# Layer-norm and RMS-norm sums with 128 columns of ones, and the gate products' copies ahead of layer norm, in a two-layer decoder trunk

## The chip, the cores and the metric

The kernel runs on one core of a Trainium2 chip. Its engines are TensorE (PE in the profile; PEld is its weight load), VectorE (DVE), ScalarE (ACT), GpSimd (POOL) and SyncE (SP), which here only starts transfers. The metric is the device time of one execution in microseconds. The time before is 1310.84 us, the median of three runs (1309.58 to 1313.38).

## The reference, cut to what matters

Two layers over 512 tokens of width 1024, all in float32. Layer 0 mixes with a causal Conformer convolution, layer 1 with differential attention; after each mixer come a SwiGLU feed-forward part and a gated embedding.

```python
u = rms_norm(h, conv_norm_g)
a = u @ w_pw1 + b_pw1                              # 1024 -> 2048
u = a[..., :D] * sigmoid(a[..., D:])
u = depthwise_causal_conv(u, dw_w, width=31) + dw_b
u = silu(layer_norm(u, ln_g, ln_b))                # mean and variance over 1024 channels
h = h + (u @ w_pw2 + b_pw2)
h = h + swiglu(rms_norm(h, ffn_norm_g), w_gate, w_up, w_down)
gate = sigmoid(rms_norm(h, ple_norm_g) @ w_ple_gate)
h = h + gate * (p[i] @ w_ple_proj)                 # "gate products" below are p[i] @ w_ple_proj
```

`rms_norm` needs the mean square over the 1024 channels of a token, `layer_norm` the mean as well.

## The kernel before, in words

Activations lie transposed: eight chunks (c = 0 to 7) of 128 channels by 512 tokens. A float32 product is made of three products in a reduced format: every operand is split into a high part (a cast on ScalarE) and a low part (a subtraction on VectorE), and `mm3` (L153 to L157) adds low weight times high data, high weight times low data, and high times high. A weight tile of 128 x 1024 comes from memory into `wraw`, and `weight` (L137) splits it into `whi` (L148) and `wlo` (L150). `ones` is a 128 x 128 tile of ones in full float32; a product in full float32 is two matmul records in the trace.

A sum over the channels of one token runs across partitions, so TensorE does it, with ones as one of its operands. There are two ways in this kernel. In the first, 128 tokens of the data are the weights and **one** column of ones is the data: the result is a column, one sum for each token (L202 and L212 for RMS norm, L441 for layer norm). In the second, ones are the weights and 512 tokens are the data: the result is a row of sums, repeated over all partitions (L442).

The convolution part goes through the chunks in one loop (L444): two products of 24 matmuls each (`half`), the gate on ScalarE and VectorE, and then the 31 taps. Chunks 1, 3, 5, 6 go through memory into an order of four phases, and TensorE does their taps with 128-column products (L357); the result goes out through memory again (`phased_out`: copy L365, a transfer on ScalarE's queue L367, four on SyncE's L370, VectorE L375). Chunk 7 shares its taps: 8 on TensorE (L313), 8 on ScalarE and GpSimd (L393, L394), 15 on VectorE (L406), joined in L407 and L409.

Layer norm follows. `moments(c)` (L420) squares a chunk on ScalarE (L429) and adds it to a running sum of squares (L433) and a running sum (L435, called `macc`), on GpSimd for all but the last. `add_moments` (L437) then makes TensorE's sums: eight one-column products and one row product for chunk 7 and the same for the running sums. From them come 1/sigma (L523 to L525, L229, L231, L529), spread over all partitions by one product with ones (`lrow`, L532), and the mean is taken off (L537, L540, L542). Per chunk follow L549 (times 1/sigma), L550 (SiLU), L552 (high part) and L554 (low part), and `linear` multiplies by `w_pw2`, its first three output chunks side by side.

The gate products of layer 0 (`factor`, L500, and `project`, L274) depend on none of this. Eight of them, 6 matmuls each, are put around layer norm to give TensorE work: four after the last tap, two after the sums, two after `lrow`. Each takes one of the four `mm` buffers of PSUM until ScalarE has copied it out (L280).

The order of instructions on each engine is set by a scheduler that plays the program through with its own costs when the kernel is built; `issue_after` ties an instruction behind another of the same engine, and `manual_schedule` (L546) keeps the written order for a block. So a change in one place can move instructions everywhere behind it.

## Time and profile before

| | |
|---|---|
| median of the runs | 1310.84 us (1309.58 to 1313.38) |
| profiled execution | 1306.01 us |
| its span, from the first instruction to the last | 1304.2 us |
| TensorE busy | 1279.5 us (98%) |
| mean granted TensorE clock | 0.988 |
| VectorE, ScalarE, GpSimd busy | 56%, 40%, 18% |
| memory traffic over the span | 100 GB/s |

How to read it: a group or timeline row gives start, busy time, engine, line, operation and `out<-in`, then the count. In brackets stands how long the engine was idle before and what released it. Where rows of one kind follow each other, the distance of their starts is the price of one; a busy time is longer than that, since matmuls overlap. "PEclk" is the share of the full clock that TensorE was granted, so a busy TensorE at 0.50 does half the work.

### The profile page before, as it was taken

How to read it: one execution, taken by the hardware profiler on the slowest of the kernel's cores; microseconds unless marked ns; L12 is line 12 of the kernel's file. 1: busy time of each engine (PE TensorE's matmuls, PEld its weight loads, DVE VectorE, ACT ScalarE, POOL GpSimd, SP SyncE). 2: the span in 40 equal slices, each digit the busy share in tenths (PEclk: the TensorE clock that was granted, in tenths of full speed). 3: DMA queues.
4: the chain of work that ended last, by engine and by line, in shares of the span. 5: the costliest groups of instructions: out<-in, count | busy, mean ns of one | idle time of the engine just before them, and what ended most of it. 6: DMA issues, size and time to landing. Idle time of an engine off the chain costs nothing. (4 is left out here: it accounts for less than half of the span.)

```text
span 1304.2 us, 15514 instructions
## 1 busy us (share of the span) xinstructions
PE 1279.5 (98%) x5960; PEld 1061.5 (81%) x5960; DVE 733.6 (56%) x1142; ACT 523.5 (40%) x827; POOL 237.9 (18%) x200
## 2 busy tenths in 40 slices
PE   9999999999999999999999998999999999999998
PEld 8888778888888888888888886778888888888887
DVE  4997566544344434356687888846543344334445
ACT  5752354332232223254566776734322233222332
POOL 1754323000000000042435635122000000000030
PEclk8999899999999999999999998999999999999999
DMA  7555214232332233233222222213332333222231
GB/s 268 189 169 181 73 34 129 97 97 97 97 97 97 97 98 97 73 124 97 84 88 92 73 65 66 72 52 109 97 98 97 97 97 97 97 97 89 85 118 65
DMA packets 46839, 131.98 MB, mean 101 GB/s; under 512 B 5379, under 2 KB 9987, under 8 KB 46764
## 3 DMA queue, kind: packets, MB, share of 16 engines
q1 hardware_dynamic: 44640, 127.55, 30.2%
q10 hardware_dynamic: 2124, 3.43, 0.9%
q8 instruction: 47, 0.77, 0.2%
q14 instruction: 28, 0.23, 0.1%
HBM read 126.75 MB, written 4.21 MB: 100 GB/s over the span
## 5 line engine op out<-in xcount | busy, mean ns | idle before, releaser
L148 ACT CAST whi<-wraw 128x1024 fp32r<-128x1024 f32 (+2 forms) x214 | 218.7, 1027 | 564.8 <-PE mm L157 384.9
L156 PE MATMUL mm<-A,whi 128*128 128x512 f32 (+1 forms) x1096 | 426.8, 391 | 1.2 <-DVE A L554 1.2
L155 PE MATMUL mm<-A,wlo 128*128 128x512 f32 (+1 forms) x1096 | 423.8, 390 | 3.4 <-DVE wlo L150 1.9
L157 PE MATMUL mm<-A,whi 128*128 128x512 f32 (+1 forms) x1096 | 424.9, 388 | 0.0
L150 DVE TENSOR_TENSOR wlo<-wraw,whi 128x1024 fp32r<-128x1024 f32 (+2 forms) x210 | 260.1, 1242 | 76.1 <-ACT whi L148 76.0
L155 PEld LDWEIGHTS mm<-A,wlo 128*128 128x128 f32 x1096 | 206.1, 188 | 47.7 <-DVE wlo L150 2.8
L156 PEld LDWEIGHTS mm<-A,whi 128*128 128x128 f32 x1096 | 206.3, 188 | 44.5 <-DVE A L554 1.5
L157 PEld LDWEIGHTS mm<-A,whi 128*128 128x128 f32 x1096 | 206.2, 188 | 42.8 <-issue 1.0
L193 POOL TENSOR_TENSOR acc<-acc,wk 128x512 f32<-128x512 f32 x35 | 56.5, 1615 | 778.1 <-issue 660.2
L156 PE MATMUL mm<-B,whi 128*128 128x512 f32 x352 | 137.5, 390 | 0.0
L157 PE MATMUL mm<-B,whi 128*128 128x512 f32 x352 | 137.4, 390 | 0.0
L155 PE MATMUL mm<-B,wlo 128*128 128x512 f32 x352 | 137.1, 391 | 0.0
L610 DVE TENSOR_TENSOR h<-mm,h 128x512 f32<-128x512 f32 x48 | 33.0, 691 | 122.9 <-PE mm L157 122.8
L602 DVE TENSOR_TENSOR big<-mm,rb 128x512 f32<-128x512 f32 x44 | 30.4, 691 | 126.2 <-PE mm L157 126.2
L600 DVE TENSOR_TENSOR big<-mm,rb 128x512 f32<-128x512 f32 x44 | 30.4, 691 | 99.4 <-PE mm L157 93.0
L157 PEld LDWEIGHTS mm<-B,whi 128*128 128x128 f32 x352 | 66.1, 188 | 14.6
L155 PEld LDWEIGHTS mm<-B,wlo 128*128 128x128 f32 x352 | 66.1, 188 | 14.3
L156 PEld LDWEIGHTS mm<-B,whi 128*128 128x128 f32 x352 | 66.1, 188 | 14.2
L157 PE MATMUL mm<-whi,A 128*128 128x512 f32 x192 | 75.6, 395 | 0.0
L156 PE MATMUL mm<-wlo,A 128*128 128x512 f32 x192 | 75.0, 396 | 0.0
L155 PE MATMUL mm<-whi,A 128*128 128x512 f32 x192 | 74.8, 396 | 0.0
L231 POOL TENSOR_TENSOR r<-v,mhalf 128x8 f32<-128x8 f32 (+1 forms) x31 | 47.4, 1528 | 148.4 <-DVE v L229 126.0
(201 smaller groups left out, 1404.9 us busy)
## 6 DMA issues: line engine op xcount, KB each, us to landing
wraw<-in_wts SPq DMA_DIRECT2D x194, 512.0 KB, 3.5
wraw<-in_wts SPq DMA_DIRECT2D x16, 384.0 KB, 3.0
D<-in_diag SPq DMA_DIRECT2D x22, 256.0 KB, 4.7
C<-in_diag SPq DMA_DIRECT2D x16, 256.0 KB, 4.8
h<-in_xT SPq DMA_DIRECT2D x8, 256.0 KB, 5.3
bias<-scr ACTq DMA_DIRECT2D x8, 256.0 KB, 3.4
out_t<-h SPq DMA_DIRECT2D x7, 256.0 KB, 2.0
wraw<-in_wts SPq DMA_DIRECT2D x4, 256.0 KB, 4.6
```

The costliest lines, as they stand in the source:

```text
L148: A.copy(hi[:, cut], raw[:, cut])
L150: eng.tensor_tensor(lo[:, cut], raw[:, cut], f(hi[:, cut]), ALU.subtract)
L155: T.matmul(acc, al, bh, start=first, stop=False)
L156: T.matmul(acc, ah, bl, start=False, stop=False)
L157: return T.matmul(acc, ah, bh, start=False, stop=last)
L193: self.last = self.eng.tensor_tensor(self.acc, self.acc, sq, ALU.add)
L231: last_pow[0] = G.tensor_tensor(r[:, :n], v[:, :n], mhalf[:, :n], ALU.pow)
L600: V.tensor_tensor(tg, pg, rb, ALU.mult)
L602: V.tensor_tensor(tu, pu, rb, ALU.mult)
L610: V.tensor_tensor(h[m], acc, h[m], ALU.add)
```

## The change

Four things are changed.

- Every per-token sum now takes **128** columns of ones as data in place of one (`columns_sum`); the reader takes the first column of each block of 128 (`first_of`). This holds for the RMS norms and for layer norm.
- Around layer norm, five gate products stand ahead of the sums in place of four, two behind them, and the last behind `lrow`. Four ties are added: the squares of chunks 6 and 7 come behind the copy of the second gate product, the last running sums (now on GpSimd) behind GpSimd's last tap, the start of GpSimd's sum for chunk 7 behind the copy of chunk 6's taps, and one tap of chunk 7 on VectorE behind the result of chunk 6. The running sums are summed by TensorE before chunk 7, not after it. The sums of squares and of values lie in two PSUM tiles, one of them in the free `sc` buffer.
- `mm3` adds high times high second and high weight times low data last.
- The splits of `w_pw2`'s tiles are tied to other places, and the third tile has a home of its own (the buffers `C5`), so its load need not wait for a `wraw` buffer.

```diff
+    def columns_sum(t, src, first, last):
+        for b in range(4):
+            cut = slice(b * P, (b + 1) * P)
+            r = T.matmul(t[:, cut], src[:, cut], ones, start=first and b == 0, stop=last and b == 3)
+        return r
+    def first_of(t):
+        return t.rearrange("p (b k) -> p b k", b=4)[:, :, 0]
...
         T.matmul(acc, al, bh, start=first, stop=False)
-        T.matmul(acc, ah, bl, start=False, stop=False)
-        return T.matmul(acc, ah, bh, start=False, stop=last)
+        T.matmul(acc, ah, bh, start=False, stop=False)
+        return T.matmul(acc, ah, bl, start=False, stop=last)
...
-                for b in range(4):
-                    T.matmul(
-                        t[:, b : b + 1], sq[:, b * P : (b + 1) * P], ones[:, 0:1],
-                        start=c + b == 0, stop=c == NC - 1 and b == 3,
-                    )
-            return rsqrt_cols(t[:, 0:4], 4, 1.0 / D)
+                columns_sum(t, sq, c == 0, c == NC - 1)
+            return rsqrt_cols(first_of(t), 4, 1.0 / D)
...
             if j == a:
-                A.activation(pacc, tap(j), AF.Identity, scale=wt(c, j), bias=col("dw_b", c))
+                with tc.issue_after(last_out[0].ins) if alone else nullcontext():
+                    A.activation(pacc, tap(j), AF.Identity, scale=wt(c, j), bias=col("dw_b", c))
...
         for j in range(b + 1, KW):
-            V.scalar_tensor_tensor(sum_, tap(j), wt(c, j), sum_, ALU.mult, ALU.add)
+            with tc.issue_after(last_shift[0].ins) if alone and j == KW - 4 else nullcontext():
+                V.scalar_tensor_tensor(sum_, tap(j), wt(c, j), sum_, ALU.mult, ALU.add)
...
         sq = sums["sq"] = wk()
-        A.activation(sq, y[c], AF.Square)
+        with tc.issue_after(last_factor[0].ins) if c > NC - 3 else nullcontext():
+            A.activation(sq, y[c], AF.Square)
         if c == NC - 1:
             return
-        eng = G if c < NC - 2 else V
-        eng.tensor_tensor(sums["acc"], sums["acc"], sq, ALU.add)
-        if c > 1:
-            eng.tensor_tensor(macc, y[1] if c == 2 else macc, y[c], ALU.add)
+        with tc.issue_after(last_pool[0].ins) if c == NC - 2 else nullcontext():
+            G.tensor_tensor(sums["acc"], sums["acc"], sq, ALU.add)
+            if c > 1:
+                G.tensor_tensor(macc, y[1] if c == 2 else macc, y[c], ALU.add)
 
     def add_moments(a, b, first, last):
-        for k in range(8):
-            src = (b if k < 4 else a)[:, k % 4 * P : (k % 4 + 1) * P]
-            last_moment[0] = T.matmul(sums["cols"][:, k : k + 1], src, ones[:, 0:1], start=first and k == 0, stop=last and k == 7)
+        columns_sum(sums["mcols"], a, first, last)
         T.matmul(sums["mean"], ones, a, start=first, stop=last)
+        last_moment[0] = columns_sum(sums["cols"], b, first, last)
...
-    for _ in range(4):
+    for m in range(5):
         factor(last_tap)
+        if m == 1:
+            last_factor[0] = last_copy[0]
...
-        add_moments(y[NC - 1], sums["sq"], True, False)
-        add_moments(macc, sums["acc"], False, True)
+        add_moments(macc, sums["acc"], True, False)
+        add_moments(y[NC - 1], sums["sq"], False, True)
...
-    for _ in range(2):
-        factor(last_product)
...
+            if c == 1:
+                factor(last_product)
...
-    linear(NC, z, add_conv, 3, first=(None, last_add[0], scaled[1]))
+    linear(NC, z, add_conv, 3, split={0: (last_add[0], None), 3: third}, home=("C5", 2))
```

How the change moves instructions is shown at three places, all around layer norm. The lines of the changed kernel are some 10 to 17 higher: L156 to L158 is `mm3`, L173 the column sums, L454 the row sums.

**TensorE, layer norm's sums.** `mm_1347` and `mm_1302` are gate products (the fourth before, the fifth now; only the last matmul of it is shown), `B_241` and `B_257` are chunk 7, `acc` is the running sum `macc`, `B_94` the running sum of squares, `wk` the squares of chunk 7. Before:

```order
L157 MATMUL mm_1347<-wtl_299,whi_1306 128x512
L441 MATMUL tp_1318<-ones_70,wk_1303 128x1 x4
L441 MATMUL tp_1318<-ones_70,B_241_1276 128x1 x4
L442 MATMUL tp_1317<-B_241_1276,ones_70 128x512
L441 MATMUL tp_1318<-ones_70,B_94_404 128x1 x4
L441 MATMUL tp_1318<-ones_70,acc_153 128x1 x4
L442 MATMUL tp_1317<-acc_153,ones_70 128x512
```

Now:

```order
L158 MATMUL mm_1302<-wtl_300,whi_1247 128x512
L173 MATMUL sc_1364<-ones_70,acc_153 128x128 x4
L454 MATMUL tp_1363<-acc_153,ones_70 128x512
L173 MATMUL sc_1364<-ones_70,B_257_1333 128x128 x4
L454 MATMUL tp_1363<-B_257_1333,ones_70 128x512
L173 MATMUL tp_1362<-ones_70,B_94_404 128x128 x4
L173 MATMUL tp_1362<-ones_70,wk_1360 128x128 x4
```

The sums start with the running sum, and the squares of chunk 7 come last.

**ScalarE, from chunk 7's taps to the gate products' copies.** `wk_1253` and `wk_1310` are the sum that GpSimd builds for chunk 7, `C_240` and `C_256` its last tap, `mm_1163` are chunk 6's taps, `B_228` is chunk 6, and the copies into `D` are those of the gate products. Before:

```order
L365 COPY big_1226<-mm_1163 128x512
L393 ACTIVATE C_240_1273<-C_226_1223,C_61_275 128x512
L367 DMA po_1228<-big_1226 128x512
L429 ACTIVATE wk_1299<-B_228_1230 128x512
L280 COPY D_254_1319<-mm_1320 128x512
L429 ACTIVATE wk_1303<-B_241_1276 128x512
L280 COPY D_256_1328<-mm_1329 128x512
```

Now:

```order
L375 COPY big_1226<-mm_1163 128x512
L402 ACTIVATE wk_1310<-C_226_1223,vec_63,C_61_275 128x512
L443 ACTIVATE wk_1352<-B_211_1103 128x512
L377 DMA po_1228<-big_1226 128x512
L405 ACTIVATE C_254_1324<-C_226_1223,C_61_275 128x512
L405 ACTIVATE C_255_1327<-C_226_1223,C_61_275 128x512
L405 ACTIVATE C_256_1330<-C_226_1223,C_61_275 128x512
L286 COPY D_239_1265<-mm_1266 128x512
L286 COPY D_241_1274<-mm_1275 128x512
L443 ACTIVATE wk_1356<-B_228_1230 128x512
```

The copy and the transfer of chunk 6 stand earlier, the start `wk_1310` of GpSimd's sum stands later (before, it was the first of ScalarE's instructions for chunk 7), and the first two copies of gate products are ahead of chunk 6's square.

**GpSimd, the same stretch.** Before:

```order
L435 TENSOR_TENSOR acc_153<-acc_153,B_211_1103 128x512
L394 TENSOR_TENSOR wk_1253<-wk_1253,C_234_1255 128x512
L394 TENSOR_TENSOR wk_1253<-wk_1253,C_235_1258 128x512
L433 TENSOR_TENSOR B_94_404<-B_94_404,wk_1295 128x512
L394 TENSOR_TENSOR wk_1253<-wk_1253,C_236_1261 128x512
L394 TENSOR_TENSOR wk_1253<-wk_1253,C_237_1264 128x512
L394 TENSOR_TENSOR wk_1253<-wk_1253,C_238_1267 128x512
L394 TENSOR_TENSOR wk_1253<-wk_1253,C_239_1270 128x512
L394 TENSOR_TENSOR wk_1253<-wk_1253,C_240_1273 128x512
L231 TENSOR_TENSOR r_268_1397<-v_267_1395,mhalf_71 128x4
```

Now:

```order
L406 TENSOR_TENSOR wk_1310<-wk_1310,C_255_1327 128x512
L406 TENSOR_TENSOR wk_1310<-wk_1310,C_256_1330 128x512
L449 TENSOR_TENSOR acc_153<-acc_153,B_228_1230 128x512
L447 TENSOR_TENSOR B_94_404<-B_94_404,wk_1356 128x512
L237 TENSOR_TENSOR r_271_1407<-v_270_1405,mhalf_71 128x4
```

Chunk 6's two running sums, which VectorE made before, are now behind the seven additions of chunk 7 on GpSimd.

More of the change, by code (lines that the diff above doesn't have):

```diff
@@ L135, in trunk, with weight @@
     loaded = [None]
-    def weight(n=1024, pieces=1, between=(), eng=V, after=None):
+    def weight(n=1024, pieces=1, between=(), eng=V, after=(None, None), home=None):
         i = wnext[0]
         wnext[0] += 1
-        raw = sb([P, 1024], "wraw", 2)
+        raw = sb([P, 1024], *(home or ("wraw", 2)))
         hi = sb([P, 1024], "whi", 4, F32R)
@@ L147, in weight @@
                 between[k]()
-            A.copy(hi[:, cut], raw[:, cut])
-            with tc.issue_after(after.ins) if after else nullcontext():
+            with tc.issue_after(after[1].ins) if after[1] else nullcontext():
+                A.copy(hi[:, cut], raw[:, cut])
+            with tc.issue_after(after[0].ins) if after[0] else nullcontext():
                 eng.tensor_tensor(lo[:, cut], raw[:, cut], f(hi[:, cut]), ALU.subtract)
@@ L200, in columns_of_chunks @@
                 A.activation(sq, h[c], AF.Square)
-                for b in range(4):
-                    T.matmul(
-                        t[:, b : b + 1], sq[:, b * P : (b + 1) * P], ones[:, 0:1],
-                        start=c + b == 0, stop=c == NC - 1 and b == 3,
-                    )
-            return rsqrt_cols(t[:, 0:4], 4, 1.0 / D)
+                columns_sum(t, sq, c == 0, c == NC - 1)
+            return rsqrt_cols(first_of(t), 4, 1.0 / D)
         def columns(self):
             t = tp()
-            for b in range(4):
-                T.matmul(t[:, b : b + 1], self.acc[:, b * P : (b + 1) * P], ones[:, 0:1], start=True, stop=True)
-            return rsqrt_cols(t[:, 0:4], 4, 1.0 / D)
+            columns_sum(t, self.acc, True, True)
+            return rsqrt_cols(first_of(t), 4, 1.0 / D)
         def diagonal(self):
@@ L279, in project @@
             step()
-        A.copy(o, acc)
+        last_copy[0] = A.copy(o, acc)
         return o
+    last_copy = [None]
     y = []
@@ L287, in trunk @@
     last_tap = [None]
+    last_out = [None]
+    last_shift = [None]
+    last_pool = [None]
     rb = None
@@ L364, in phased_out @@
         o = big()
-        A.copy(o, accs[c])
+        last_out[0] = A.copy(o, accs[c])
         d = dram.tile([P, S], F32, tag=f"po{c}", name=f"po{c}")
@@ L393, in other_taps @@
                 A.activation(pr, tap(j), AF.Copy, scale=wt(c, j))
-                G.tensor_tensor(pacc, pacc, pr, ALU.add)
+                last_pool[0] = G.tensor_tensor(pacc, pacc, pr, ALU.add)
         yc = sb([P, 2, S], f"B{c}", 1)
@@ L491, in trunk @@
             moments(c - 3)
-    pe_taps(NC - 1)
-    other_taps(NC - 1)
-    for c in range(NC - 3, NC):
-        moments(c)
     pp = []
+    pw = [weight(), weight()]
     def factor(after):
@@ L510, in factor @@
             pp.append(project(ph, m, pw[m // 4], o))
-    pw = [weight(), weight()]
-    sums["mean"], sums["cols"] = tp(), tp()[:, 0:8]
-    for _ in range(4):
+    pe_taps(NC - 1)
+    for m in range(5):
         factor(last_tap)
+        if m == 1:
+            last_factor[0] = last_copy[0]
+    other_taps(NC - 1)
+    for c in range(NC - 3, NC):
+        moments(c)
+    sums["cols"], sums["mean"], sums["mcols"] = tp(), tp(), sc()
     with tc.issue_after(last_product[0].ins):
-        add_moments(y[NC - 1], sums["sq"], True, False)
-        add_moments(macc, sums["acc"], False, True)
+        add_moments(macc, sums["acc"], True, False)
+        add_moments(y[NC - 1], sums["sq"], False, True)
     for _ in range(2):
@@ L522, in trunk @@
     vs = sb([P, P // 2], "v8", 2)[:, :8]
-    V.tensor_scalar(vs, sums["cols"], 1.0 / D, None, ALU.mult)
+    V.tensor_scalar(vs[:, 4:8], first_of(sums["mcols"]), 1.0 / D, None, ALU.mult)
     V.tensor_tensor(vs[:, 4:8], vs[:, 4:8], vs[:, 4:8], ALU.mult)
-    V.tensor_tensor(vs[:, 0:4], vs[:, 0:4], vs[:, 4:8], ALU.subtract)
+    V.scalar_tensor_tensor(vs[:, 0:4], first_of(sums["cols"]), 1.0 / D, vs[:, 4:8], ALU.mult, ALU.subtract)
     r = rsqrt_cols(vs[:, 0:4], 4, 1.0)
@@ L548, in trunk, with linear @@
             if c < NC:
-                scaled.append(V.tensor_tensor(y[c], y[c], lrow, ALU.mult))
+                V.tensor_tensor(y[c], y[c], lrow, ALU.mult)
                 A.activation(y[c], y[c], AF.Silu, scale=col("ln_g", c), bias=col("ln_b", c))
                 z.append((sb([P, S], f"A{2 * c}", 1, F32R), sb([P, S], f"A{2 * c + 1}", 1, F32R)))
-                A.copy(z[c][0], y[c])
+                hi = A.copy(z[c][0], y[c])
             if c >= 2:
-                V.tensor_tensor(z[c - 2][1], y[c - 2], f(z[c - 2][0]), ALU.subtract)
-    def linear(n_in, src, consume, group0=1, before=None, after=None, first=(None,) * 3):
+                lo = V.tensor_tensor(z[c - 2][1], y[c - 2], f(z[c - 2][0]), ALU.subtract)
+            if c == 1:
+                factor(last_product)
+            if c == 3:
+                third = lo, hi
+    def linear(n_in, src, consume, group0=1, before=None, after=None, split={}, home=None):
         m = 0
@@ L561, in linear @@
             g = group0 if m == 0 else 1
-            ws = [weight(n_in * P, after=first[i] if m == 0 else None) for i in range(g)]
+            ws = [weight(n_in * P, after=split.get(m, (None, None)), home=home if m + i == 2 else None) for i in range(g)]
             accs = [mm() for _ in range(g)]
```

6 lines of the change are left out of this document (3 added, 3 removed).

## The prediction

> **What bounds the kernel now.** I read the page first, then the table by stage, then TensorE's timeline where that table shows a slow clock or idle time.
>
> ```profile
> span 1304.2 us, 15514 instructions
> PE 1279.5 (98%) x5960; PEld 1061.5 (81%) x5960; DVE 733.6 (56%) x1142; ACT 523.5 (40%) x827; POOL 237.9 (18%) x200
> PEclk8999899999999999999999998999999999999999
> ```
>
> TensorE is the bound: 1279.5 of 1304.2 us. Only three things can be gained: its 24.7 us of idle time, the slices in which its clock is below 9, and work taken off it. The table by stage (columns: length, busy time of PE, PEld, DVE, ACT, POOL, then clock and memory) says where the first two lie.
>
> ```profile
> 30.00:125.00 95.00, 95.00 (x526) 81.91 (x525) 82.62 (x100) 45.58 (x62) 54.84 (x42) 1.00 0.53 172
> 153.00:174.00 21.00, 19.32 (x66) 14.24 (x65) 8.81 (x14) 10.01 (x19) 8.28 (x6) 0.68 0.10 29
> 174.00:640.00 466.00, 465.60 (x2055) 383.39 (x2056) 228.16 (x278) 156.43 (x202) 40.13 (x28) 1.00 0.30 96
> 640.00:870.00 230.00, 216.15 (x1128) 182.43 (x1126) 177.81 (x461) 149.91 (x336) 92.81 (x89) 0.98 0.22 71
> 800.00:805.00 5.00, 1.83 (x10) 1.01 (x8) 4.91 (x12) 4.60 (x12) 1.43 (x3) 0.98 0.09 26
> 805.00:810.00 5.00, 1.92 (x7) 1.67 (x8) 4.62 (x16) 2.47 (x8) 2.63 (x2) 0.50 0.70 236
> 815.00:820.00 5.00, 2.41 (x17) 1.95 (x15) 4.37 (x9) 3.72 (x7) 1.95 (x1) 1.00 0.50 150
> ```
>
> The feed-forward stretch has nothing to give. The losses are layer norm (153 to 174: a clock of 0.68 means that 21 x 0.32 = 6.7 us were lost, 13.4 us at half speed), attention (640 to 870, 13.9 us idle, 8.8 of them in the three rows after 800), and a first one, where the norm of the input is summed:
>
> ```profile
> 19.71 3.40 PE L202 MATMUL tp<-ones,wk 128*128 128x1 f32 x30
> 22.97 0.65 PE L155 MATMUL mm<-A,wlo 128*128 128x512 f32 x1
> 23.42 3.41 PE L202 MATMUL tp<-ones,wk 128*128 128x1 f32 x16
> 26.69 0.77 PE L156 MATMUL mm<-A,whi 128*128 128x512 f32 x1
> 30.12 0.40 PE L155 MATMUL mm<-A,wlo 128*128 128x512 f32 x1
> 23.00:24.00 1.00, 1.00 (x6) 0.91 (x6) 0.00 (x0) 0.81 (x1) 0.00 (x0) 0.56 0.06 25
> ```
>
> Thirty one-column records take 22.97 - 19.71 = 3.26 us, 0.109 each. After them the clock halves although TensorE was busy all the time, and sixteen more take 23.42 to 26.69, 0.204 each. So the clock does not follow the busy time; a stretch of one-column products counts as rest.
>
> **The change part by part.**
>
> *128 columns for one.* The trace has products of 128 columns in full float32, the taps L357, and of 512 columns, L313:
>
> ```profile
> 130.29 4.18 PE L357 MATMUL mm<-C,D 128*128 128x128 f32 x36
> 134.30 1.95 PE L357 MATMUL mm<-C,C 128*128 128x128 f32 x16
> L357 PEld LDWEIGHTS mm<-C,D 128*128 128x128 f32 x40 | 4.8, 192 | 0.1
> 138.32 7.03 PE L313 MATMUL mm<-C,D 128*128 128x512 f32 x16
> 144.79 0.79 PE L155 MATMUL mm<-wth,wlo 128*128 128x512 f32 x1
> 146.57 0.39 PE L155 MATMUL mm<-wth,wlo 128*128 128x512 f32 x1
> 149.07 0.39 PE L157 MATMUL mm<-wtl,whi 128*128 128x512 f32 x1
> ```
>
> Each L357 record has a weight tile of its own, as the sums have, and 36 take 4.01 us: 0.111. So a sum with 128 columns costs what one with one column costs; 136 records (64 of the first norm, 32 of layer norm, 40 of the other norms) times 0.002 is 0.3 us. And the row of 30 to 125, in which three more such runs of taps lie (chunks 1, 3 and 5), has a clock of 1.00, so I expect 128-column sums to keep it. From 22.97 to 30.12 the first norm now takes 7.15 us for one product, sixteen sum records and eight products. A reduced product is (149.07 - 146.57)/11 = 0.227. At full clock that is 9 x 0.227 + 16 x 0.111 = 3.8 us. **Gain 3.3 us.** It arrives at layer norm only if VectorE keeps up: in 30 to 125 TensorE never waits and VectorE has 12.4 us free, so I count it whole.
>
> [...]
>
> *Layer norm.* I lay the changed order over the old times, as if the first norm had not moved.
>
> ```profile
> 151.49 0.50 PE L155 MATMUL mm<-wth,wlo 128*128 128x512 f32 x1 [2.03 <-ACT D L280]
> 154.07 1.87 PE L441 MATMUL tp<-ones,wk 128*128 128x1 f32 x8 [0.72 <-ACT wk L429]
> 174.40 0.50 PE L156 MATMUL mm<-A,whi 128*128 128x512 f32 x1 [1.19 <-DVE A L554]
> 137.93 2.55 ACT L393 ACTIVATE C<-C,C 128x512 f32<-128x512 f32 x4
> 142.12 0.57 ACT L365 COPY big<-mm 128x512 f32<-128x512 f32 x1
> 143.90 0.33 ACTq L367 DMA_DIRECT2D po<-big  x1
> 150.34 0.63 ACT L429 ACTIVATE wk<-B 128x512 f32<-128x512 f32 x1 [5.78 <-DVE B L375]
> 150.87 0.57 ACT L280 COPY D<-mm 128x512 f32<-128x512 f32 x1
> 137.94 10.26 DVE L406 SCALAR_TENSOR_TENSOR sc<-C,C,sc 128x512 f32<-128x512 f32 x13
> 149.21 1.09 DVE L375 SCALAR_TENSOR_TENSOR B<-B,vec,shrow 128x512 f32<-128x512 f32 x1 [1.01 <-DMA B<-po]
> 138.71 2.63 POOL L394 TENSOR_TENSOR wk<-wk,C 128x512 f32<-128x512 f32 x2 [2.15 <-ACT C L393]
> 142.54 6.72 POOL L394 TENSOR_TENSOR wk<-wk,C 128x512 f32<-128x512 f32 x5
> 141.30 1.28 POOL L433 TENSOR_TENSOR B<-B,wk 128x512 f32<-128x512 f32 x1
> ```
>
> The 2.03 us came from ScalarE: its copy L280 stood behind the square of chunk 6, which waited for VectorE and a transfer. Now two copies are ahead of that square. ScalarE does four taps (to 139.8), the copy of chunk 6's taps (140.4), the start of GpSimd's sum (0.7: 141.1) and a square (141.7); then the transfer goes out, 2.2 us earlier, and as it took 149.21 - 143.90 = 5.3 us, chunk 6 is there at 147.0. The first two copies are done by 148.1, before the fourth and fifth product need their buffers (149.3 on), so five products run without a wait. The first three took 144.79 to 149.07 + 0.23, two more are 12 x 0.227: 152.0.
>
> What is late next is GpSimd: its sum for chunk 7 starts at 141.1 instead of 138.7. Seven additions at 1.34 and a square's at 1.28 end at 151.8, and `macc` (1.28) is ready at 153.1, the sum of squares at 154.4. VectorE: ten taps to 145.8, chunk 6 from 147.0 to 148.1, four taps at 0.79 to 151.3, L407 after GpSimd at 151.8, L409: chunk 7 at 153.1. So TensorE waits **1.1 us** at the head of the sums, with the two gate products and all that follows queued behind. Then 0.9 for four columns of `macc`, 0.8 for its row (L313: 6.47/16 = 0.40 a record), 0.9 and 0.8 for chunk 7, 0.9 and 0.9 for the squares: 158.4. Two gate products of 6 x 0.227 end at 161.1.
>
> ```profile
> 162.81 0.17 DVE L523 TENSOR_SCALAR v<-tp 128x8 f32<-128x8 f32 x1 [8.32 <-PE tp L441]
> 164.71 1.28 ACT L529 ACTIVATE wk<-ident,r 128x128 f32<-128x128 f32 x4 [8.29 <-POOL r L231]
> 169.22 1.88 DVE L549 TENSOR_TENSOR B<-B,tp 128x512 f32<-128x512 f32 x3 [0.84 <-PE tp L532]
> 169.95 0.82 ACT L550 ACTIVATE B<-B,vec 128x512 f32<-128x512 f32 x1 [1.00 <-DVE B L549]
> ```
>
> The chain from sums to spread took 162.81 to 165.99, 3.2 us; two of its four small steps on VectorE now need only `macc` and chunk 7, done before. 158.5 + 2.9 = 161.4, and a gate product's copy holds ScalarE to 160.3 before it, so 161.6: a wait of **0.5 us**. Spread to 162.4; last gate product to 163.8. Chunk 0 needs L549 (0.73 to its SiLU, by the rows), 0.72 and 0.62 from 162.7 on: 164.8, a wait of **1.0 us**. The low part of chunk 0 is done 0.7 later, and is used after six products (1.4 us): the 1.19 us before 174.40 is gone. The three weight splits cost nothing: they now lie in the 8.32 us in which VectorE was idle (without that cover 1.2 us each).
>
> In the old order the three low-weight products of this group were done when TensorE went on at 174.40; now they are at 164.8 + 0.7 = 165.5. **Gain 8.9 us**: 6.7 of the clock, 3.9 of old waits (2.03, 0.72, 1.19) less 2.6 of new ones, and 0.9 that I take to lie in the changes between kinds of products, which are longer at half clock. Later chunks come every 1.4 us on ScalarE and are used every 2.0 us.
>
> *mm3's order and the third tile's home.* No row in 174 to 640 shows a wait for a moving low part, so 0. But the scheduler has replayed the attention part: the end of attention has the same steps, with the projection's products before or after their neighbours. There the trace can't say. A wait there is about 2.5 us (three rows with 8.8 us), and a slow stretch behind it costs 1.7 us: the clock was halved for 13.4 us in layer norm and from 23.1 to just before 30.12, about 6.8, so I estimate steps of 3.4 us. One such wait less or more makes -4.2 to +4.2 us. I take 0, as the tail begins with the same list of stages left.
>
> Sum: -3.3 - 8.9 + 0.2 = **-12.0 us** (0.1 of the 0.3 lies in the terms). The profiled execution, 1306.0 us with 1.8 around its span, becomes 1294; the runs' median lies 4.8 above that execution, and the change is carried over to it: 1310.8 - 12 = **1299 us**.
>
> **The rivals.**
>
> 1. *The clock follows idle time, not the width.* Then the waits start the slow stretches and the sums only lie in them. [...] For it: 2.03 us idle stood ahead of the fall at 152.9. Against it: no idle time ahead of the fall at 23.1. The first 3.3 us would stay lost, and my 1.1 us wait would halve the clock again: 32 sum records at 0.204 and four row records at 0.81 take 9.8 us for 5.3, and two gate products at half speed 1.4 us more. Of 8.9 us some 3 are left: **1308**. A weaker form, one slow step of 3.4 us after the wait, costs 1.7 us and is in my range.
>
> 2. *Slower: load and stream add up.* Place: the 136 sum records. Price: between 0.109 (the pace of loads) and 0.192 (the length of one L357 load, L202's alike) for the load, plus 0.40/4 = 0.10 for the stream, so 0.10 to 0.18 more each: 13.7 to 25 us against 12.0 gained, **1313 to 1324**. It decides from 0.09 more per record. Against it: the 36 records in 4.01 us.
>
> 3. *Attention's new order loses.* One or two more waits of 2.5 us with a slow stretch: +4 to +8, 1303 to 1307; three or more would undo the gain. For it: VectorE and ScalarE are at 4.9 and 4.6 of 5 us there, so any instruction placed badly is late at once. Against it: QKV's products cover 640 to 800.
>
> 4. *It wins*: one wait less, 1291 to 1295.
>
> **How the numbers follow.** Forecast (1295 to 1303) 0.66; rival 1 0.06; its weak form or a later `macc` (1302 to 1305) 0.06; rival 2 0.03; rival 3 0.12 with 0.02 of it over 1315; rival 4 0.07. The likeliest is 1299. From 1293 to 1306 lie forecast, weak form, most of 3 and half of 4: about 0.84. What this measurement tells from no change is 0.3%, 3.9 us, so faster means below 1306.9: forecast, weak form, 4 and 0.08 of 3, 0.87. Same: rival 1 and a little of 3, 0.08. Slower: rival 2 and what is left of 3, 0.05.
>
> **What would show it.** Right: clock 1.00 from 20 to 30 us and (some 3 us earlier than now) from 150 to 165; L173 records at 0.11; one wait of about 1 us for GpSimd ahead of L173 on `acc`; small ones before L548 and the first product with `A`; `linear` starting near 161.5. Wrong: a clock of 0.50 in either place (rival 1), L173 at 0.2 and full clock (rival 2), more idle in 640 to 870 than the 13.9 us now (rival 3).

## The result, and the profile after

The change is faster: **1302.17 us** median of 20 runs (1298.51 to 1308.21), against 1310.43 us (1303.9 to 1314.92) for the kernel before in as many. The ratio is 0.9942 with a 95% interval of 0.9926 to 0.9957, so 7.6 us. The forecast was 1299 with a range of 1293 to 1306: the sign was right and the median lies inside the range, but the gain is 7.6 us and not the 12 that were added up.

The profiled execution took 1301.05 us, 5.0 less than the one before. Its page, and its table by stage (columns as before: length, busy time of PE, PEld, DVE, ACT, POOL, clock, memory):

```profile
span 1299.3 us, 15533 instructions
PE 1273.9 (98%) x5960; PEld 1055.8 (81%) x5960; DVE 733.8 (56%) x1140; ACT 522.4 (40%) x827; POOL 238.0 (18%) x202
PEclk9999999999999999999999997999999999999999
```

```profile
20.00:30.00 10.00, 10.00 (x67) 9.05 (x67) 3.23 (x4) 3.98 (x5) 2.74 (x2) 1.00 0.50 175
30.00:125.00 95.00, 94.09 (x520) 80.73 (x519) 83.64 (x101) 46.00 (x64) 55.51 (x42) 1.00 0.54 174
150.00:171.00 21.00, 17.54 (x85) 12.86 (x85) 15.54 (x23) 12.14 (x22) 11.01 (x9) 1.00 0.16 51
637.00:864.00 227.00, 212.81 (x1106) 178.53 (x1105) 176.98 (x459) 146.00 (x332) 89.16 (x89) 0.97 0.22 70
795.00:809.00 14.00, 9.04 (x26) 7.28 (x27) 11.36 (x32) 8.34 (x19) 6.30 (x7) 0.52 0.55 170
863.00:868.00 5.00, 4.38 (x12) 3.47 (x13) 2.79 (x2) 1.95 (x3) 4.77 (x3) 0.66 0.52 147
```

Both slow stretches that the prediction spoke of are gone: the clock is 1.00 at the first norm and in layer norm. Attention is worse: 14.2 us of idle time, about as before (13.9), but 795 to 809 now runs at 0.52, and behind it, at 863, comes a slow stretch that was not there. TensorE's timeline has the prices and waits, VectorE's what stands behind the largest of layer norm:

```profile
24.33 1.95 PE L173 MATMUL tp<-ones,wk 128*128 128x128 f32 x16
26.04 0.48 PE L158 MATMUL mm<-A,whi 128*128 128x512 f32 x1
113.36 4.25 PE L367 MATMUL sc<-C,D 128*128 128x128 f32 x36 [0.80 <-DMA C<-pi]
152.11 1.16 PE L173 MATMUL sc<-ones,acc 128*128 128x128 f32 x8 [1.00 <-POOL acc L449]
160.90 1.13 PE L548 MATMUL tp<-wk,ones 128*128 128x512 f32 x2 [0.48 <-ACT wk L545]
165.39 0.50 PE L156 MATMUL mm<-A,wlo 128*128 128x512 f32 x1 [1.98 <-ACT A L565]
863.62 0.59 PE L156 MATMUL mm<-A,wlo 128*128 128x512 f32 x1 [3.03 <-DVE wlo L151]
```

```profile
160.75 0.58 ACT L551 ACTIVATE wk<-tp 128x512 f32<-128x512 f32 x1
161.36 1.89 DVE L554 SCALAR_TENSOR_TENSOR B<-tp,B 128x512 f32<-128x512 f32 x3 [3.29 <-ACT wk L551]
163.17 1.87 DVE L562 TENSOR_TENSOR B<-B,tp 128x512 f32<-128x512 f32 x3
```

Sixteen sum records with 128 columns take 26.04 - 24.33 = 1.71 us, 0.107 each: no dearer than with one column (0.109).

Where the 5.0 us come from shows when TensorE's `mm3` products are counted in both timelines and the starts of the same number are compared:

| product | where | before | after | gained so far |
|---|---|---|---|---|
| 60th | behind the first norm's sums | 30.59 | 28.17 | 2.4 |
| 360th | convolution, chunk 6 | 124.62 | 123.55 | 1.1 |
| 600th | behind layer norm | 211.71 | 203.63 | 8.1 |
| 2340th | ahead of attention | 610.83 | 602.73 | 8.1 |
| 3300th | behind attention | 912.69 | 907.78 | 4.9 |

So in these two executions layer norm gave 7.0 us, the first norm 1.1, and attention took 3.2 back.

One more number is used below. Each run is recorded with its span and its mean granted clock; (1 - clock) x span is the time lost to the clock. For the kernel before it is 17.5 us (mean of 29 runs recorded with the first experiments, 1309.6 us in the mean), for the change 10.3 us (its 20 runs, 1302.4). The times differ by 7.2 us, the losses by 7.1: as far as these means can tell (each is uncertain by about 0.6), **the whole gain is clock**. This loss is a measure and not a price: it counts idle time inside a slow stretch too, and a kernel can lose more of it without being slower (columns_32 below). Inside the change's 20 runs the loss goes from 6.5 to 14.4 us and follows the time (correlation 0.92).

### The profile page after: what moved, and what is told of

Same layout as the page of the kernel before. It is cut to its first block, busy times and chain, and to the rows that moved or that the text cites. A ratio compares the mean times of both kernels' runs of the same rounds, so it can differ in the third digit from the quotient of the medians.

```text
span 1299.3 us, 15533 instructions
## 1 busy us (share of the span) xinstructions
PE 1273.9 (98%) x5960; PEld 1055.8 (81%) x5960; DVE 733.8 (56%) x1140; ACT 522.4 (40%) x827; POOL 238.0 (18%) x202
## 4 chain that ended last, share of the span: by engine, by line
PE 84%; DVE 5%; DMA 3%; POOL 3%; ACT 2%; issue 2%; SPq 0%; POOLq 0%; DVEq 0%; ACTq 0%
PE mm L156 27%; PE mm L158 26%; PE mm L157 26%; POOL wk L406 2%; DVE wlo L151 1%; DMA wraw<-in_wts 1%; DVE sc L418 1%; PE mm L846 1%; DMA po<-big 1%; PE sc L810 1%; PE tp L830 1%; PE sc L811 1%; PE tp L173 0%; ACT A L180 0%; ACT whi L149 0%
## 5 line engine op out<-in xcount | busy, mean ns | idle before, releaser
L156 PE MATMUL mm<-A,wlo 128*128 128x512 f32 (+1 forms) x1096 | 428.5, 391 | 6.7 <-DVE wlo L151 3.0
L158 PE MATMUL mm<-A,whi 128*128 128x512 f32 (+1 forms) x1096 | 422.6, 389 | 0.0
L156 PEld LDWEIGHTS mm<-A,wlo 128*128 128x128 f32 x1096 | 206.4, 188 | 51.0 <-DVE wlo L151 3.5
L158 PEld LDWEIGHTS mm<-A,whi 128*128 128x128 f32 x1096 | 205.9, 188 | 42.5 <-issue 0.5
L156 PE MATMUL mm<-B,wlo 128*128 128x512 f32 x352 | 137.8, 391 | 0.0
L158 PE MATMUL mm<-B,whi 128*128 128x512 f32 x352 | 137.4, 390 | 0.0
L158 PEld LDWEIGHTS mm<-B,whi 128*128 128x128 f32 x352 | 66.1, 188 | 14.5
L156 PEld LDWEIGHTS mm<-B,wlo 128*128 128x128 f32 x352 | 66.1, 188 | 14.3
L156 PE MATMUL mm<-whi,A 128*128 128x512 f32 x192 | 75.9, 396 | 0.0
L158 PE MATMUL mm<-wlo,A 128*128 128x512 f32 x192 | 74.7, 396 | 0.0
```

Of the source, the lines that this page charges most:

```text
L156: T.matmul(acc, al, bh, start=first, stop=False)
L158: return T.matmul(acc, ah, bl, start=False, stop=last)
```

## The experiments

| kernel | median, us | ratio to the kernel before | lost to the clock, mean us |
|---|---|---|---|
| the change | 1302.2 | 0.9942 (0.9926 to 0.9957) | 10.3 |
| width_alone | 1301.8 | 0.9949 (0.9930 to 0.9967) | 10.2 |
| order_alone | 1308.8 | 0.9999 (0.9975 to 1.0024) | 19.8 |
| first_one | 1308.8 | 0.9992 (0.9972 to 1.0013) | 15.0 |
| columns_32 | 1300.8 | 0.9925 (0.9896 to 0.9955) | 13.3 |
| columns_64 | 1298.2 | 0.9914 (0.9880 to 0.9948) | 8.7 |
| old_product_order | 1298.9 | 0.9924 (0.9896 to 0.9951) | 7.3 |
| projection_old_order | 1300.3 | 0.9923 (0.9899 to 0.9947) | 8.9 |
| splits_untied | 1302.3 | 0.9942 (0.9924 to 0.9959) | 9.0 |
| chunk7_first | 1299.1 | 0.9921 (0.9897 to 0.9945) | 9.5 |
| best | 1295.9 | 0.9893 (0.9871 to 0.9915) | 5.8 |
| best2 | 1295.0 | 0.9886 (0.9859 to 0.9913) | 6.9 |
| best2_first_one | 1301.5 | 0.9940 (0.9918 to 0.9963) | 11.7 |

Where two rows are compared, half-widths are combined as the root of the sum of squares; 0.001 is 1.3 us.

### width_alone: the 128 columns without the rest

```diff
 (kernel before)
-                for b in range(4):
-                    T.matmul(t[:, b : b + 1], sq[:, b * P : (b + 1) * P], ones[:, 0:1], ...)
+                columns_sum(t, sq, c == 0, c == NC - 1)      # likewise in columns() and add_moments()
```

> The kernel before with one part of the change alone: all norm sums by products with 128 columns of ones; gate products, ties, splits, product order and the buffer for the third weight stay as before. Width theory: the clock is full from 20 to 30 us and from 150 to 166 us although the 2.03 us wait ahead of the sums stays; the first norm gives 2.4 us of which about 1.1 is lost again before 115 us, layer norm gives the 6.7 us of its slow clock: together -8 us, ratio 0.994. Rival (the clock follows the idle time in front of it): the fall behind the 2.03 us wait stays, only the first norm's 1.3 us is left: ratio 0.999.

0.9949: within the noise (3.2 us) the width alone gives what the change gives. Its table by stage, and two rows of TensorE's timeline:

```profile
20.00:30.00 10.00, 10.00 (x65) 8.95 (x64) 3.22 (x4) 3.35 (x4) 3.07 (x2) 1.00 0.45 171
149.00:167.00 18.00, 14.53 (x71) 10.37 (x69) 10.99 (x18) 11.47 (x21) 8.69 (x6) 1.00 0.16 55
167.00:175.00 8.00, 6.84 (x18) 5.37 (x19) 7.77 (x12) 6.42 (x10) 0.56 (x1) 0.57 0.27 75
148.45 0.50 PE L155 MATMUL mm<-wth,wlo 128*128 128x512 f32 x1 [1.46 <-ACT D L285]
164.60 0.97 PE L155 MATMUL mm<-A,wlo 128*128 128x512 f32 x3 [2.28 <-ACT A L557]
```

The sums run at full clock. The run does not put the rival's question, though: the wait ahead of them is 1.46 us here and not the 2.03 of before, and behind the first norm no wait of up to 1.75 us that stood alone was followed by a slow stretch in any profile (counted under the rivals below). The waits of the first linear products (2.28 us and two more, 0.91 and 1.18) stand ahead of a slow stretch of their own, 167 to 175. In this execution layer norm gave only 1.2 us (gained at the 360th product 2.5, behind layer norm 3.6).

### order_alone: the new order with one column

```diff
 (the change)
-            r = T.matmul(t[:, cut], src[:, cut], ones, start=first and b == 0, stop=last and b == 3)
+            r = T.matmul(t[:, b : b + 1], src[:, cut], ones[:, 0:1], start=first and b == 0, stop=last and b == 3)
```

> The changed kernel with its sums put back to products with one column of ones; everything else of the change stays (four of the sums' five places in TensorE's order included). Width theory: the first norm's slow stretch is back (7 us at half clock), and layer norm's sums start one too; the shorter waits (3.9 us less 3.5) give next to nothing: ratio 0.998 to 1.001. Rival: the clock at layer norm stays full, since no wait of 2 us stands ahead of the sums: ratio 0.994 to 0.996.

0.9999, as the width theory said; the loss to the clock, 19.8 us, is above that of the kernel before. In its profile the slow stretches ahead of the linear layer are these:

```profile
7.00:19.00 12.00, 10.38 (x31) 8.39 (x31) 9.45 (x12) 10.15 (x17) 0.00 (x0) 0.57 1.04 395
28.00:36.00 8.00, 8.00 (x31) 7.01 (x31) 4.22 (x4) 2.09 (x3) 3.96 (x3) 0.57 0.30 96
147.00:152.00 5.00, 5.00 (x9) 2.11 (x8) 4.78 (x7) 4.14 (x8) 1.64 (x2) 0.66 0.14 52
168.00:172.00 4.00, 4.00 (x13) 3.21 (x13) 0.33 (x2) 1.06 (x3) 1.02 (x1) 0.57 0.36 135
```

In 28 to 36 TensorE is busy for 8.00 of 8.00 us, behind 32 one-column records that begin at 24.40. The stretch of 7 to 19 begins behind the first eight such records, in a wait of 1.62 us; the profile of the kernel before had nothing there. The one of 147 to 152 stands behind a wait of 1.95 us. In layer norm the sums lie at 162.8 to 168.1 at full clock, with row products between them, and one step follows. Another, at 178.6, stands behind the 1.99 us wait of the first linear product.

### first_one and best2_first_one: one column at the first norm alone

```diff
 (the change, and the fastest version below)
-                columns_sum(t, sq, c == 0, c == NC - 1)
-            return rsqrt_cols(first_of(t), 4, 1.0 / D)
+                for b in range(4):
+                    T.matmul(t[:, b : b + 1], sq[:, b * P : (b + 1) * P], ones[:, 0:1], ...)
+            return rsqrt_cols(t[:, 0:4], 4, 1.0 / D)
```

> The changed kernel with one column of ones again in the first norm's sums alone. The prediction counted the first norm's 3.3 us whole at the end: then this is 3.3 us slower than the changed kernel, ratio 0.9965 to 0.997 against before. The theory formed since: what TensorE gains at the first norm ends in the wait ahead of the layer-norm sums, since macc is ready at 152 to 153 us whatever TensorE did; the run with 32 columns reached layer norm 3.6 us later and had a wait of 0.20 instead of 1.0 to 2.4 us. Then this is 0 to 1.5 us slower than the changed kernel: ratio 0.994 to 0.9955.

> The same edit in the fastest version, where chunk 7 no longer waits for chunk 5's transfer and TensorE runs into layer norm's sums without a wait. Theory: there nothing absorbs it, so the slow stretch behind the first norm's sums costs its whole 3.3 us or more: ratio 0.991 to 0.9915 against before, where the fastest version had 0.9886. Rival (the first norm's slow stretch is hidden in both): ratio 0.9885 to 0.9895.

My theory, that this gain ends in a later wait, fell. first_one is 0.0050 slower than the change: 6.5 us, with 3.4 either way. In the fastest version it is 0.0054, 7.0 us with 4.6 either way. By these medians the first norm's width is worth about twice the 3.3 us of the prediction, and nearly all that the change gains. Each interval alone still holds 3.3; the two together do not (6.7 us, with 2.7 either way). Why it may be more than the profile of before showed:

```profile
8.00:13.00 5.00, 4.41 (x16) 3.70 (x17) 3.90 (x6) 5.00 (x10) 0.00 (x0) 0.66 1.05 407
25.00:33.00 8.00, 8.00 (x31) 6.88 (x30) 4.27 (x4) 2.14 (x3) 3.96 (x3) 0.57 0.36 100
159.00:163.00 4.00, 4.00 (x17) 2.97 (x17) 4.00 (x4) 1.10 (x2) 0.97 (x1) 0.57 0.17 35
```

As in order_alone, there is an early stretch as well. Where the steps fall differs between executions: of the four profiles with one column at the first norm these two have an early stretch, those of the kernel before and of best2_first_one have the later one alone, and none of the ten with wider sums has an early one.

Two further comparisons can be read from the table. first_one against the kernel before holds all that the change does except the first norm: 1.0 us gained, with 2.7 either way. first_one against order_alone holds the width in layer norm and in the other norms: 0.9 us, with 4.2 either way. So for layer norm the runs show no gain from the width that is clear of noise, though the time lost to the clock is 4.8 us smaller.

### columns_32 and columns_64: how narrow is too narrow?

```diff
 (the change; 64 likewise)
-            r = T.matmul(t[:, cut], src[:, cut], ones, ...)
+            r = T.matmul(t[:, b * P : b * P + 32], src[:, cut], ones[:, 0:32], ...)
```

> The changed kernel with 32 columns of ones in each norm sum instead of 128; a record should still take 0.11 us, as with 1 and with 128. Theory (the clock follows the part of the time in which columns stream): 32 columns are a quarter of the work of 128 in the same time, so a run of 30 such records counts as rest and the clock halves near 23 us, as with one column. Rival (only the very shortest products count as rest): clock 1.00 there, time as the changed kernel.

> The changed kernel with 64 columns of ones in each norm sum. With 32 the clock halved behind the first norm's sums, with 128 it stayed. [...] Rival (any product shorter than 128 counts as rest): as 32 columns in every run.

First columns_32, then columns_64:

```profile
20.00:24.00 4.00, 4.00 (x31) 3.72 (x29) 0.00 (x0) 1.75 (x3) 0.00 (x0) 1.00 0.60 240
24.00:32.00 8.00, 8.00 (x33) 7.12 (x33) 3.66 (x4) 2.02 (x3) 3.10 (x2) 0.57 0.23 63
```

```profile
20.00:32.00 12.00, 12.00 (x75) 10.70 (x74) 3.22 (x4) 4.60 (x6) 4.52 (x3) 1.00 0.43 148
153.00:158.00 5.00, 5.00 (x20) 3.60 (x21) 4.63 (x6) 1.10 (x2) 1.02 (x1) 0.66 0.36 98
152.85 1.10 PE L173 MATMUL sc<-ones,acc 128*128 128x64 f32 x8 [2.37 <-POOL acc L449]
```

With 32 columns the first norm's slow stretch is there, with 64 it is not, and TensorE is busy all the time in both (26 records take 2.82 us in either, 0.108 each). So in these two profiles the width decides and not the busy time. The loss with 64 columns (8.7 us) is not above that of 128 (10.3) and below that of 32 (13.3), so between 64 and 128 columns no edge showed, and the rival (as 32 columns in every run) falls. The kernel with 32 columns was nevertheless not slower than the change (four runs). In its one profile it is 3.0 us behind the change after layer norm, and 2.8 us of that are made up between the 2340th product and attention's output projection; I cannot say by what. columns_64 falls in layer norm, but behind a wait of 2.37 us.

### old_product_order and projection_old_order: the order of mm3

```diff
 (the change; everywhere, or in attention's output projection alone)
-        T.matmul(acc, ah, bh, start=False, stop=False)
-        return T.matmul(acc, ah, bl, start=False, stop=last)
+        T.matmul(acc, ah, bl, start=False, stop=False)
+        return T.matmul(acc, ah, bh, start=False, stop=last)
```

> The changed kernel with the three products of a weight in their old order (low x high, high x low, high x high). Theory: a record costs the same whichever stands next to it, so nothing: within 1 us of the changed kernel (ratio 0.993 to 0.996 against before). Rival: two products in a row with the same weight tile are cheaper, or the first product waits less for the low split: the old order loses more than 2 us (ratio above 0.996).

> The changed kernel with the old order of the three products in one layer alone, attention's output projection. Theory: with the low part of the input last, the four sums that wait for the last head all end together, so the weights' buffers and VectorE's additions come 1.3 us later (3.03 us of waiting at 863.6 in the changed kernel, 1.75 in the kernel before and with the old order everywhere), and the longer wait halves the clock for one step of 3.4 us (1.7 us): 3.0 us faster than the changed kernel, ratio 0.9915 to 0.993 against before, with a wait of 1.75 us and no slow clock behind it. Rival: the 2.4 us that the old order gained everywhere came from another place or from chance: ratio 0.994, as the changed kernel.

The prediction gave the product order nothing. The old order everywhere measured 0.9924, 0.0018 below the change (-0.0050 to +0.0014; 3.3 us by the medians), in the one layer 0.9923 (-0.0048 to +0.0010). These intervals include zero, so the times alone don't decide. The traces show what the order does in that layer. First old_product_order, then projection_old_order, each with the clock behind the row:

```profile
864.40 0.50 PE L156 MATMUL mm<-A,wlo 128*128 128x512 f32 x1 [1.75 <-DVE wlo L151]
863.00:870.00 7.00, 5.60 (x25) 4.64 (x26) 4.80 (x5) 3.58 (x6) 4.74 (x3) 1.00 0.44 150
```

```profile
866.94 0.50 PE L156 MATMUL mm<-A,wlo 128*128 128x512 f32 x1 [1.75 <-DVE wlo L151]
866.00:872.00 6.00, 5.06 (x22) 4.17 (x23) 3.85 (x4) 3.12 (x5) 4.74 (x3) 1.00 0.50 163
```

All seven kernels with the new order in that layer (the change, order_alone, first_one, splits_untied, chunk7_first, columns_32, columns_64) wait 3.02 or 3.03 us there, and in six of their profiles a step at half clock follows (not in that of columns_64); all seven with the old order wait 1.75, with no step behind it. The low part of the last head comes late. In the old order only the second of three products needs it, and the four sums end one after the other; in the new one all four wait with their last product. First the kernel before, from the first product that uses the last head, then the change:

```profile
865.39 1.20 PE L155 MATMUL mm<-A,wlo 128*128 128x512 f32 x4 [0.78 <-ACT A L169]
867.09 1.89 DVE L926 TENSOR_TENSOR h<-mm,h 128x512 f32<-128x512 f32 x3 [0.96 <-PE mm L157]
868.89 1.21 DVE L150 TENSOR_TENSOR wlo<-wraw,whi 128x1024 fp32r<-128x1024 f32 x1
```

```profile
857.58 0.50 PE L156 MATMUL mm<-A,wlo 128*128 128x512 f32 x1 [0.78 <-ACT A L180]
859.95 2.48 DVE L943 TENSOR_TENSOR h<-mm,h 128x512 f32<-128x512 f32 x4 [1.64 <-PE mm L158]
862.36 3.44 DVE L151 TENSOR_TENSOR wlo<-wraw,whi 128x1024 fp32r<-128x1024 f32 x2
```

The split starts 3.5 us after that product before, 4.8 in the change: 1.3 us later, and the step at half clock behind it (0.66 in 863 to 868) costs 1.7, together 3.0. All fourteen profiles agree: from this product to the 3300th it takes 47.3 to 47.4 us in the seven with the old order, 50.2 in the six with the new order and the step, and 48.65 in columns_64, without the step. So the new order costs 2.9 us there, of the 3.2 that attention took. What stands ahead of the layer varies more than that between executions (250.9 to 256.9 us from the 2340th product on), which may be why the runs' times do not show it clearly.

### splits_untied: the weight splits where the scheduler puts them

```diff
 (the change)
-    linear(NC, z, add_conv, 3, split={0: (last_add[0], None), 3: third}, home=("C5", 2))
+    linear(NC, z, add_conv, 3)
```

> The changed kernel with the three weight splits of the first linear layer free to run where the scheduler puts them, and the third weight back in the common pair of load buffers. Theory: they stand in VectorE's queue ahead of chunk 7's last taps; VectorE waits 2.2 us for GpSimd there, so one split of 1.2 to 1.6 us is free and a second delays chunk 7 by at most 1 us, and the later load of the third weight costs up to 1 us: 0 to 2 us slower than the changed kernel (ratio 0.994 to 0.996 against before). Rival: VectorE is what sets the end of layer norm's input, and the splits cost their full 3 to 4 us (ratio 0.997).

0.9942, the change's own ratio; the rival's 0.997 is outside the interval. So this part of the change is worth nothing that can be measured. The profile shows something else, a step at half clock behind a wait although all sums have 128 columns:

```profile
150.00:153.00 3.00, 0.68 (x4) 0.26 (x4) 2.07 (x4) 0.66 (x1) 2.92 (x4) 1.00 0.00 0
153.00:157.00 4.00, 4.00 (x17) 2.97 (x17) 2.02 (x2) 1.10 (x2) 0.94 (x1) 0.57 0.15 45
152.77 1.57 PE L173 MATMUL sc<-ones,acc 128*128 128x128 f32 x7 [2.32 <-POOL acc L449]
```

### chunk7_first: what makes macc late

In the change, VectorE takes chunk 5's taps, which come back through memory, ahead of chunk 7's gate, and waits for them at the head of its queue:

```profile
132.65 1.12 DVE L385 SCALAR_TENSOR_TENSOR B<-B,vec,shrow 128x512 f32<-128x512 f32 x1 [4.26 <-DMA B<-po]
134.40 1.32 DVE L498 SCALAR_TENSOR_TENSOR C<-big,vec,big 128x512 f32<-128x512 f32 x1
139.65 1.27 POOL L406 TENSOR_TENSOR wk<-wk,C 128x512 f32<-128x512 f32 x1 [4.47 <-ACT wk L402]
```

```diff
 (the change; the running sum of chunk 5 is tied behind the first of GpSimd's additions)
+        if c == NC - 3: late.append(shift)          # phased_out: chunk 5's L385 is kept back
+            if alone and j == b + 4: late.pop()()   # other_taps: behind chunk 7's fourth tap
-                with tc.issue_after(last_out[0].ins) if alone else nullcontext():
+                if True:                            # start of GpSimd's sum, no longer behind chunk 6's copy
```

> The changed kernel with one edit at chunk 7: VectorE takes chunk 5's added-up taps (which come back through a transfer) behind chunk 7's gate and first four taps instead of ahead of them, and ScalarE starts GpSimd's sum of chunk 7 without waiting for the copy of chunk 6. Theory: VectorE stood 4.26 us (5.97 and 6.06 in two other runs) at the head of its queue for that transfer, with chunk 7 queued behind it, and this sets when macc is ready, 152 to 153 us whatever TensorE gained before; so chunk 7 starts about 4 us earlier, macc is ready before 148 us, and TensorE's wait ahead of the layer-norm sums (1.00 us in the changed kernel, 2.3 in others) is gone: 1.0 to 2.4 us faster than the changed kernel, ratio 0.9925 to 0.993 against before. Rival: GpSimd's additions (1.27 to 1.45 us each, nine of them) or chunk 6's transfer set macc's time, and the wait stays above 0.8 us: ratio 0.994.

0.9921, 1299.1 us: 3.0 us less by the medians (the intervals of the two overlap). In its profile the gate's product is at 128.54, GpSimd starts at 130.89, the running sum is ready at 145.7, and the sums begin at 149.35 with no wait, where the change waited 1.00 us and five other kernels 2.3 to 2.4. Of the 8.8 us by which GpSimd starts earlier, 5.9 are the gate's; the other 2.9 lie between the gate and GpSimd's start, where the edit drops a tie as well:

```profile
128.54 0.75 DVE L514 SCALAR_TENSOR_TENSOR C<-big,vec,big 128x512 f32<-128x512 f32 x1
130.89 2.63 POOL L415 TENSOR_TENSOR wk<-wk,C 128x512 f32<-128x512 f32 x2 [7.30 <-ACT C L414]
144.41 1.29 POOL L465 TENSOR_TENSOR acc<-acc,B 128x512 f32<-128x512 f32 x1 [0.95 <-DVE B L389]
149.35 1.05 PE L173 MATMUL sc<-ones,acc 128*128 128x128 f32 x8
```

The wait for that transfer differs between executions: 4.26 us on VectorE in the change, 5.5 to 6.5 in the five kernels that wait 2.3 to 2.4 us for `macc`.

### best and best2: what helps, together

```diff
 (best and best2: old mm3 order but in layer norm's linear layer; the mean's negative early)
+    drow = wk()
+    A.mul(drow, sums["mean"], -1.0 / D)             # right behind add_moments, ahead of two gate products
+                with tc.issue_after(last_v[0].ins):  # VectorE's subtractions behind the small steps
 (best alone)
-POOL_TAPS = (10, 0, 11, 0, 11, 0, 0, 8)
+POOL_TAPS = (10, 0, 11, 0, 11, 0, 0, 7)
+            with tc.issue_after(last_pool[0].ins) if c == NC - 1 else nullcontext():
                 G.memset(up[:, :PAD], 0.0)
 (best2 alone: chunk7_first's edit in their place)
```

> The changed kernel with four edits: the new order of the three products in layer norm's linear layer alone; ScalarE takes the mean's negative from PSUM as soon as it is there, ahead of the gate product's copy, and VectorE's three subtractions stand behind the sum's small steps; one tap of chunk 7 goes from GpSimd to VectorE; GpSimd's fill of the last padding stands behind its sum of chunk 4. Theory: 3.0 us (out-projection), about 1 us of the 1.00 us wait for macc, 1.3 us of the 1.98 us wait of the first linear product, and up to 1.1 us of what is lost before 115 us: 5 to 6 us faster than the changed kernel, ratio 0.990 against before. Rival: what layer norm gains is given back in attention, whose order moves with every edit: ratio 0.992 to 0.993, as the old order alone.

> All that helped, together: the changed kernel with the new product order in layer norm's linear layer alone, the mean's negative taken early with VectorE's subtractions behind the small steps, and chunk 7 ahead of chunk 5's transfer (no tap moved, the fill of the padding where the changed kernel has it). Theory: 3 us of the out-projection, 1.1 us of the first linear product's wait, 1.0 to 2.4 us of the sums' wait: 5 to 6.5 us faster than the changed kernel, ratio 0.989 to 0.990, and the sums start without a wait before 151.5 us. Rival: the chunk's earlier start collides with the transfers of chunk 6 and gives nothing: ratio 0.991.

best came to 0.9893, as forecast, but two of its four edits did nothing: the wait ahead of the sums was still 1.00 us, and the one for chunk 5's transfer at 113.23 was 1.20 (0.80 in the change). One tap less could not help, since GpSimd began chunk 7 at 141.70 (139.65 in the change). The early mean cut the first linear product's wait from 1.98 to 0.89 us. best2, with chunk 7 first, has the lowest median of this study (not clear of that of best): 1294.95 us, 14.6 below the kernel before beside it, 7 below the change. In its profile:

```profile
148.00:162.00 14.00, 12.68 (x66) 9.44 (x64) 9.25 (x16) 6.82 (x15) 6.66 (x7) 1.00 0.23 76
162.06 0.50 PE L156 MATMUL mm<-A,wlo 128*128 128x512 f32 x1 [0.91 <-ACT A L583]
860.16 0.50 PE L156 MATMUL mm<-A,wlo 128*128 128x512 f32 x1 [1.75 <-DVE wlo L151]
```

## Why the prediction was right, and where it was wrong

**The mechanism was right, shown for the first norm.** Behind a stretch of one-column products the clock fell there (0.51 from 24 to 30 us in the kernel before, 0.57 from 25 to 33 in first_one, 1.00 from 20 to 30 in the change): the width alone costs 6.5 and 7.0 us in two pairs of kernels. The sums with 128 columns cost 0.107 us each and ran at full clock at both places in the change's profile; the mean gain over the runs is clock. For layer norm the same cause is not shown to be the main one. In the kernel before, the clock falls at 152.82, 1.3 us behind the 2.03 us wait and ahead of the first narrow sum at 154.07:

```profile
153.00:154.00 1.00, 0.35 (x1) 0.00 (x0) 1.00 (x2) 0.61 (x2) 0.00 (x0) 0.50 0.00 0
```

So the wait is the likelier start of that stretch, and the narrow sums may have kept it up.

**First norm, 3.3 us: too small, and carried badly.** In the profile pair it was 2.4 at 30 us; over the runs it is 6.5 (first_one). The step that failed is the reading of one execution: "from 22.97 to 30.12" was the short form of a loss that in other profiles has an early stretch as well. "I count it whole" was wrong in the profile pair too: 1.1 was left at 125 us. Of the 1.3 lost on the way, 1.0 went around a wait of 0.80 us of TensorE for chunk 5's transfer, in a stretch in which I had said that it never waits. Its cause I haven't settled: it is there in seven of the fourteen profiles, with 0.49 to 1.20 us, and not in the others.

**Layer norm, 8.9 us: 7.0 in this execution, by most of the terms named, but a lucky execution.** The wait for `macc` was 1.00 (predicted 1.1), that ahead of the spread product 0.48 (0.5), the low part's 1.19 gone as said. The first linear product waited 1.98 instead of 1.0, which is half of what is missing; the other 0.9 I haven't located. No run shows the 0.9 us that the sum put into longer changes between kinds of products at half clock: in the kernel before, the sums ran at half clock from 154.07 to the next product at 163.70, 9.6 us, and 32 records at 0.204 with four at 0.81 make 9.8. (`linear` so started at 165.39 and not near 161.5; 2.2 us of that are the first norm's gain that did not arrive.) I had the scaling of chunk 0 follow the spread product; VectorE's three subtractions (1.89 us) stand between, and they started only behind ScalarE's copy of the mean at 160.75, which stood behind the spread's diagonal. best, which takes that copy early, waits 0.89.

That the 1.1 us for `macc` came true was luck. Between the 360th and the 600th product, five other kernels with wide sums in layer norm and its new order (old_product_order, splits_untied, projection_old_order, columns_64, first_one) gained 2.3 to 3.2 us in their profiles and not 7.0: they waited 2.32 to 2.38 us for `macc`, and in four of them a step at half clock followed. The five in which that wait was 0 to 1.0 us (best, columns_32, chunk7_first, best2, best2_first_one) gained 6.4 to 9.3. The step that failed is the time of `macc`: I took it from one trace, and it goes with VectorE's wait for chunk 5's transfer, 4.3 us in the change and 5.5 to 6.5 in the five that waited longer.

Whether width and order are separate terms, as my sum had them, the traces don't settle: width_alone gained 1.2 us in layer norm and order_alone 0.9 (6.1 us behind the kernel before at the 360th product, 5.3 behind layer norm), both together 7.0 in the change and 2.3 to 3.2 in those five.

**Product order and attention, 0 with bounds of 4.2: wrong by 2.9 us for a reason that could be found.** I looked for a wait for a low part between 174 and 640 and found none; the layer where the low part comes late is the output projection, and the wait for `wlo` behind it (1.75 at 870.16) stands in the profile of the kernel before. Rival 3 (1303 to 1307) came near in size, with the wrong cause: not the scheduler's new order but `mm3`'s. The other 0.3 of attention's 3.2 is one execution's.

**The rivals.** Rival 1, as it stood, is out by first_one and best2_first_one, where the width alone changes the time. Its weak form is true beside the forecast. I counted TensorE's waits in the fourteen profiles from 100 us on, without 640 to 845 us (attention). Waits of 0.9 to 1.75 us that stood alone were followed by a step at half clock in none of sixteen, those of 1.95 to 2.03 us in six of ten, those of 2.28 to 2.50 us in five of seven, those of 3.02 or 3.03 us in six of seven. So 1.95 us were enough in some executions. Rival 2 is out: 0.107 a record.

**The sum.** By the runs it reads: first norm -6.5, product order about +3 (by the traces), and layer norm some -4. That last is what the 1.0 us of first_one against the kernel before leaves, so it is uncertain by 2.7 at least. Terms that were off by 3, 3 and 5 us cancelled in part: that the range held is partly luck.

## What to carry to other kernels

Here a TensorE that was busy for 8.00 of 8.00 us ran at a clock of 0.57 behind sums of one and of 32 columns: look at the clock behind runs of one-column products, and widen them where that costs nothing (0.107 us a record with 128 columns, 0.109 with one). Where a product order is changed, ask in which layer its last operand is late, and which buffers wait for all sums to end. And where a queue's head waits for a transfer through memory, put ready work of the next chunk ahead of it (here it took the wait for `macc` away; the gain in time is not clear of noise).

A term that rests on the clock could not be sized from one execution here (the change lost 6.5 to 14.4 us to it in 20 runs): (1 - clock) x span of every run gives its mean and its spread.

## What the runs showed of the hardware

- At the first norm the clock halved for 6.83 us behind sums of one column (0.109 us a record) and of 32 (0.108), while TensorE was busy for 8.00 of 8.00 us; with 64 (0.108) and 128 columns (0.107) it stayed at 1.00 (one profile each for 32 and 64).
- The time lost to the clock comes in steps: in the fourteen traces' clock records the slow stretches are 3.41, 6.83, 10.24 or 13.65 us long (but for one at the end of each trace), and inside one trace their starts lie whole multiples of 3.41 us apart. The grid lies elsewhere in each trace, and the same kernel (the change) loses 6.5 to 14.4 us in different runs.
- The end of attention is the largest clock loss that is left: 0.52 for 14 us in the change. No experiment was made there.
